# Two transformer blocks in split float32: every SBUF tile begun at a multiple of 128 bytes

## The chip, the cores and the metric

The kernel runs on one core of one Trainium2 chip. The metric is the device time of one execution in microseconds (us), lower is better. The core has five engines with queues of their own: TensorE (PE; its weight loads are listed apart as PEld), VectorE (DVE), ScalarE (ACT), GpSimd (POOL) and SyncE (SP, which issues most of the transfers). A tile of SBUF, the memory on the chip, has up to 128 partitions, and "where a tile begins" is its byte address within each partition.

## The reference, cut to what matters

512 tokens of width 1024 pass two blocks. The first mixes tokens by forgetting attention and gated linear attention, then attends to 256 memory rows, then runs a squared-relu MLP of width 4096. The second runs a SwiGLU layer of width 2816, a mixer of differential attention and of attention over compressed, selected and windowed keys, another SwiGLU layer and a last norm.

```
h = x + parallel_mixer(rms_norm(x, norm_mix_g), ...)          # fox attention | gla, then @ w_out
h = h + memory_cross_attention(rms_norm(h, ...), rms_norm(mem, ...), ...)
u = jax.nn.relu(rms_norm(h, norm_mlp_g) @ mlp_w1)
h = h + (u * u) @ mlp_w2
x = x + 0.5 * swiglu(rmsnorm(x, ffn1_norm), w1, w3, w2)       # (silu(h @ w1) * (h @ w3)) @ w2
x = x + token_mix(rmsnorm(x, mix_norm), w_in, ...)
      # merged = sigmoid(g_a) * (y_da @ w_proj_da) + sigmoid(g_b) * (y_ns @ w_proj_nsa);  merged @ w_out
x = x + 0.5 * swiglu(rmsnorm(x, ffn2_norm), w1, w3, w2)
return rmsnorm(x, final_norm)
```

## The kernel before, in words

Activations are held transposed, 8 tiles of 128 features by 512 tokens. To keep float32's precision at TensorE's single-pass rate, each operand is split into two fp32r tiles: a high part (a copy by ACT) and a low part (DVE subtracts the high part from the full value). A product is then three matmuls: high by high, high by low, low by high. The trace writes fp32r as fp32 or f32. A plain float32 matmul stands as two records there, an fp32r matmul as one.

- `wsub` loads a piece of weights of up to 128x1024 floats (512 KB) into one of 3 `wraw` buffers by SP's queue, and splits every 512 columns of it into one of 4 `wspl` buffers.
- `lin` makes a product with the activations as moving operand: the 128x128 stationary operand comes from `wspl`, the moving operand is 512 columns of x (normed input), u (hidden layer of a MLP), y or z (outputs of attention). `nat` is the other way round: 256 columns of `wspl` move, and 128 columns of x are stationary.
- `norm` makes the tiles x0h, x0l to x7h, x7l in the pool `xp`, which has one buffer for each name, and the norm's factors `rstdb` and `rstdn`.
- Attention streams (`fox`, `gla`, `xattn`, `da`, `nsa`) are woven with streams of projections, so that TensorE has products while a softmax runs on ACT and DVE.

The order on each engine comes from a scheduler that simulates the program's time; the tiles' buffers set what waits for what. Pools are laid out one behind the other, tile behind tile, in steps of 32 bytes. In the built kernel before, the tiles begin this many bytes past a multiple of 128: x, wspl, wraw, misc and nsv 64; u, dav, xv and y (but for four of y in the first mixer, 64) 32; z, kbh and the residual h 96; ones, gc, ident, identr, identb and maskb 0.

At the start, `warm` fills TensorE's wait for the first data with 16 matmuls of `ones` by `ones` (plain float32, 128 columns); then come the gate projection `misc` (64 output rows, over x0 to x7) and the first `nat` products.

Of the kernel before, what the change touches and what calls it, by code (L numbers as in the profile page):

```python
# [31 lines left out]
NGC = _c  # L32


def weave(main, fill, ratio=1.0, lead=0.0):
    """Emit two streams in turn. Each yields the tensor engine's time of what it has emitted, or a
    predicate that the other stream has to make true first."""
# [23 lines left out]
def both(*gens):  # L61
    """generators in turn, in one stream: the second two steps for each of the others"""
    live = [[g, 1] for i, g in enumerate(gens) if g is not None]
    while live:
        for x in list(live):
            for _ in range(x[1]):
                try:
                    v = next(x[0])
                except StopIteration:
                    live.remove(x)  # L70
                    break
                if v is not LATER:
                    yield v


def pipe(gens):
    """generators in one stream, each cut into stages by LATER: a stage comes after the next
    generator's stage before it"""
# [27 lines left out]

class Net:
# [16 lines left out]
    # ---------------------------------------------------------------- small helpers  # L124
# [34 lines left out]
    # ---------------------------------------------------------------- weights  # L159
    def wsub(self, ap, keep=None):  # L160
        """one piece [128, kt, n] of a weight, as its two exact parts: (h, l) of every [128, n]"""
# [18 lines left out]
    def lin(self, w, X, n=S, m=128, parts=None, bank="lin"):  # L180
        """[m, n] = (columns of w)^T X^T; w [128, kt, m] in DRAM, X a list of pairs (None: not yet there)"""
        kt = w.shape[1]
        ps = self.ps(bank)
        i = 0
# [15 lines left out]
    def nat(self, w, X, ntok, evac):  # L200
        """[tok, 256] = X w for w [2, 128, 4, 256]"""
# [14 lines left out]
    # ---------------------------------------------------------------- norms  # L216
    def rsqrt(self, ps, m, d):
        """[128, m]: (ps / d + eps) ** -0.5, with a Newton step"""
# [12 lines left out]
    def token_rsqrt(self, sqs, n, d, sel):  # L231
        """1 / rms over the rows of sqs (per column of sel) of every token; [128 tok, (tile, column)]"""
# [9 lines left out]
    def spread(self, r, n):  # L242
        """[128, n tok] from [128 tok, tile], in PSUM"""
# [11 lines left out]
    def norm(self, h, g, n=S, pool=None, spool=None, first=False):  # L255
        """h: 8 tiles [128, n]; parts of h*g; 1/rms of every token on all partitions, and by token"""
# [28 lines left out]
        rn = spool.tile([128, n // 128], F32, name="rstdn")  # L285
# [3 lines left out]
    def out_proj(self, w, Y, scale=None, banks=("lin",)):  # L289
        """h += (Y w) * scale"""  # L290
# [7 lines left out]
    # ---------------------------------------------------------------- attention pieces  # L298
    def softmax(self, ps, dst, factor=None, scale=True):
        """rows of exp(s - max), times 1/sum (and factor) unless told not to; returns 1/sum"""  # L300
# [18 lines left out]
    def pt(self, P, kbs):  # L319
        """transposed column blocks of a causal P, as parts; where each block begins"""  # L320
# [14 lines left out]
    def av(self, o, P, passes, first, last):  # L335
        """o += sum over key blocks; passes(kb) = [(stationary, part of P)]"""
# [20 lines left out]
    def stacks(self, hi, lo, pool):  # L357
        """[q_hi; q_lo] of the two heads of a tile"""
# [7 lines left out]
    def dup(self, t, U):  # L366
        """each half of the rows on both halves"""
# [5 lines left out]
    def fold(self, ps, dst):  # L373
        """dst [64 rows] = the two halves of an output with parts of V"""
# [4 lines left out]
    def head_tiles(self, w, X, rn, pool, gate, done):  # L379
        """4 heads of 64 columns, by token: 1/rms of each; then transposed, as 2 tiles of 2 heads in PSUM"""  # L380
# [33 lines left out]
    def rope(self, src, dst):  # L414
        """dst = src * cos + (halves swapped) * (-sin, sin)"""
# [12 lines left out]
    # ---------------------------------------------------------------- the whole  # L428
    def run(self):
        tc, nc, a = self.tc, self.nc, self.a  # L430
        with ExitStack() as ctx:
            def pool(name, bufs, c=ctx, side=None):
                kw = {"side": side} if side else {}
                return c.enter_context(tc.tile_pool(name=name, bufs=bufs, **kw))
# [13 lines left out]
            self.small = pool("small", 8)  # L448
            self.stat = pool("stat", 1)
            self.spill = ctx.enter_context(tc.tile_pool(name="spill", bufs=1, space=bass.MemoryType.DRAM))  # L450
            hctx = ExitStack()
            self.hp = pool("hp", 1, hctx, "right")
# [31 lines left out]
    def setup(self):  # L484
# [3 lines left out]
        self.gc = self.const.tile([128, NGC], F32, name="gc")  # L488
        nc.sync.dma_start(self.gc, a["gcols"])
        one = self.const.tile([128, 1], F32, name="one")  # L490
        self.act(one, self.ones[:, 0:1], AF.Exp)
# [14 lines left out]
    def warm(self, n):  # L506
        """keeps the tensor engine's clock up while the first data comes"""
        for _ in range(n):
            self.mm(self.ps("tr")[:, :128], self.ones, self.ones, True, True)

    def late_setup(self):
# [7 lines left out]
        self.gx = self.const.tile([128, 3], F32, name="gx")  # L519
# [3 lines left out]
        self.dah = self.const.tile([128, 8], F32, name="dah")  # L523
# [3 lines left out]
    # ---------------------------------------------------------------- block 1: fox and gla  # L527
    def mixer(self):
        a = self.a
        self.warm(16)  # L530
# [41 lines left out]
    def rowsel(self, pool, rows):  # L572
        """[rows, 8, 128]: -1 where the row is h mod 32"""
# [6 lines left out]
    def log_sigmoids(self, srcs):  # L580
        """log_sigmoid(src + bias) of some (src, bias, rows); all exponentials before the logarithms"""
# [13 lines left out]
    def fox_in(self, X, rb, rn, p1, p2, y, misc):  # L595
        """projections of fox: gates, then keys, queries and values"""
# [3 lines left out]
        def gates():  # L600
# [22 lines left out]
            # log decay of gla, cumulated in every chunk  # L623
# [76 lines left out]
    def gla_proj(self, i, X, rb, rn, p1):  # L700
        """queries, keys and values of two heads of gla"""
# [18 lines left out]
        dd = p1.tile([128, 8], F32, name=f"gdc{i}")  # L720
# [87 lines left out]
    # ---------------------------------------------------------------- block 1: cross attention  # L808
# [104 lines left out]
    # ---------------------------------------------------------------- block 1: mlp  # L913
# [736 lines left out]
```

## Time and profile before

| | |
|---|---|
| three timed runs | 2293.12, 2302.83, 2303.39 us; median 2302.83 |
| profiled execution, first to last instruction | 2294.0 us |
| PE busy | 2256.5 us (98%), 11507 matmul records |
| PEld busy | 1864.0 us (81%) |
| DVE, ACT, POOL busy | 1269.5, 970.9, 245.1 us (55, 42, 11%) |
| chain that ended last, by engine | PE 94%, DVE 2%, ACT 2%, DMA 1%, issue 1% |
| the same by line | `lin` 78%, s 7%, o 4%, transposes 2% |

The chain is followed back from the last instruction, at each step to what released it; its shares say what the time hangs on. No time of the profiled execution other than its span is listed; the span lies 0.9 us above the fastest timed run and 8.8 us below the median. A matmul's start is recorded, its end is modelled, so the rate of a stream is read from starts, not from the duration of one.

### The profile page before, as it was taken

What the parts mean: (1) busy time and instruction counts of PE and PEld (TensorE: products, weight loads), DVE (VectorE), ACT (ScalarE), POOL (GpSimd) and SP (SyncE); (2) the same over time, 40 slices, a digit from 0 to 9 for tenths busy, and PEclk for the clock granted to TensorE, in tenths of its full rate; (3) what the DMA queues carried; (4) which work ended last, traced back from release to release, by engine and by line L of the source; (5) the groups of instructions that cost most, each with busy time, mean ns of one, the idle gap of its engine ahead of it and who ended that gap; (6) DMA issues with size and microseconds to landing.
All of it is one profiled execution on the core that took longest, in us unless ns stands there. A gap on an engine that the chain in (4) does not pass through costs nothing.

```text
span 2294.0 us, 30689 instructions
## 1 busy us (share of the span) xinstructions
PE 2256.5 (98%) x11507; PEld 1864.0 (81%) x11507; DVE 1269.5 (55%) x2397; ACT 970.9 (42%) x1937; POOL 245.1 (11%) x301
## 2 busy tenths in 40 slices
PE   8999999999999999999999999999999999999998
PEld 7887799888888888888878778878877788888887
DVE  6655566655335445435456666677784555543543
ACT  6553355444234333323343334456676334332333
POOL 2201012100000000000002112143441000000000
PEclk9999999999999999999999999999999999999999
DMA  4331133222323322233345455422121322223222
GB/s 141 93 102 51 60 125 107 67 93 93 97 96 95 98 93 92 89 104 99 95 137 134 141 156 139 126 63 62 56 56 63 112 95 99 92 91 102 97 92 79
DMA packets 79268, 222.62 MB, mean 97 GB/s; under 512 B 11536, under 2 KB 19632, under 8 KB 79120
## 3 DMA queue, kind: packets, MB, share of 16 engines
q1 hardware_dynamic: 78480, 220.01, 30.9%
q8 instruction: 90, 1.47, 0.3%
q10 hardware_dynamic: 576, 0.52, 0.1%
q14 instruction: 58, 0.48, 0.1%
q0 software_dynamic: 64, 0.13, 0.0%
HBM read 189.69 MB, written 4.19 MB: 85 GB/s over the span
## 4 chain that ended last, share of the span: by engine, by line
PE 94%; DVE 2%; ACT 2%; DMA 1%; issue 1%; SPq 0%; POOL 0%; ACTq 0%; DVEq 0%; POOLq 0%
PE lin L129 78%; PE s L129 7%; PE o L129 4%; PE tr L326 2%; PE tr L129 2%; DMA wraw<-in_n_vda 0%; ACT P L138 0%; DVE wspl L132 0%; DMA wraw<-in_t_kda 0%; ACT wspl L138 0%; DVE nm L302 0%; ACT pth L138 0%; DVE ta L132 0%; DMA wraw<-in_t_c 0%; ACT L138 0%
## 5 line engine op out<-in xcount | busy, mean ns | idle before, releaser
L138 ACT ACTIVATE wspl<-wraw 128x512 fp32r<-128x512 f32 (+1 forms) x677 | 421.9, 626 | 893.5 <-PE lin L129 802.0
L132 DVE TENSOR_TENSOR wspl<-wraw,wspl 128x512 fp32r<-128x512 f32 (+1 forms) x677 | 469.0, 696 | 442.0 <-ACT wspl L138 434.9
L225 POOL TENSOR_TENSOR rqr<-rqv,mhalf 128x4 f32<-128x4 f32 (+1 forms) x21 | 20.5, 977 | 1386.2 <-DVE rqv L224 1348.7
L129 PE MATMUL lin<-x0h,wspl 128*128 128x512 f32 (+2 forms) x396 | 157.6, 399 | 2.8 <-ACT wspl L138 1.0
L129 PE MATMUL lin<-x7h,wspl 128*128 128x512 f32 (+2 forms) x396 | 153.7, 389 | 0.0
L129 PE MATMUL lin<-x1h,wspl 128*128 128x512 f32 (+2 forms) x396 | 153.7, 389 | 0.0
L129 PE MATMUL lin<-x4h,wspl 128*128 128x512 f32 (+2 forms) x396 | 153.5, 389 | 0.0
L129 PE MATMUL lin<-x6h,wspl 128*128 128x512 f32 (+2 forms) x396 | 153.2, 388 | 0.0
L129 PE MATMUL lin<-x5h,wspl 128*128 128x512 f32 (+2 forms) x396 | 153.2, 388 | 0.0
L129 PE MATMUL lin<-x3h,wspl 128*128 128x512 f32 (+2 forms) x396 | 152.8, 387 | 0.0
L138 ACT ACTIVATE P<-s,nm 128x128 f32<-128x128 f32 (+2 forms) x224 | 117.3, 527 | 83.6 <-DVE nm L302 68.1
L129 PE MATMUL lin<-x2h,wspl 128*128 128x512 f32 (+2 forms) x396 | 152.7, 387 | 0.0
L302 DVE TENSOR_REDUCE nm<-s 128x1 f32<-128x128 f32 (+3 forms) x208 | 105.0, 509 | 53.9 <-PE s L129 52.5
L138 ACT ACTIVATE pth<-tr 128x512 fp32r<-128x512 f32 x152 | 76.4, 529 | 46.4 <-PE tr L326 36.7
L132 DVE TENSOR_TENSOR ptl<-tr,pth 128x512 fp32r<-128x512 f32 x152 | 88.2, 596 | 12.5 <-ACT pth L138 10.5
L129 PEld LDWEIGHTS lin<-x0h,wspl 128*128 128x128 f32 (+1 forms) x396 | 74.9, 189 | 17.4 <-ACT wspl L138 4.2
L129 PEld LDWEIGHTS lin<-x2h,wspl 128*128 128x128 f32 (+1 forms) x396 | 74.5, 188 | 15.2
L129 PEld LDWEIGHTS lin<-x1h,wspl 128*128 128x128 f32 (+1 forms) x396 | 74.8, 189 | 14.8
L129 PEld LDWEIGHTS lin<-x7h,wspl 128*128 128x128 f32 (+1 forms) x396 | 74.4, 188 | 14.8 <-issue 0.2
L129 PEld LDWEIGHTS lin<-x3h,wspl 128*128 128x128 f32 (+1 forms) x396 | 74.3, 188 | 14.9
L129 PEld LDWEIGHTS lin<-x4h,wspl 128*128 128x128 f32 (+1 forms) x396 | 74.5, 188 | 14.6 <-issue 0.2
L129 PEld LDWEIGHTS lin<-x5h,wspl 128*128 128x128 f32 (+1 forms) x396 | 74.4, 188 | 14.5 <-issue 0.2
(705 smaller groups left out, 5550.8 us busy)
## 6 DMA issues: line engine op xcount, KB each, us to landing
wraw<-in_t_m SPq DMA_DIRECT2D x64, 512.0 KB, 3.8
wraw<-in_t_f1a SPq DMA_DIRECT2D x22, 512.0 KB, 3.5
wraw<-in_t_f1b SPq DMA_DIRECT2D x22, 512.0 KB, 3.5
wraw<-in_t_f2a SPq DMA_DIRECT2D x22, 512.0 KB, 3.5
wraw<-in_t_f2b SPq DMA_DIRECT2D x22, 512.0 KB, 3.5
qu<-r SPq DMA_DIRECT2D x80, 128.0 KB, 2.3
wraw<-in_t_f1c SPq DMA_DIRECT2D x16, 512.0 KB, 3.4
wraw<-in_t_f2c SPq DMA_DIRECT2D x16, 512.0 KB, 3.5
```

The source lines that it names most:

```text
L129: self.nc.tensor.matmul(out, lhsT, rhs, start=start, stop=stop, **kw)
L132: self.nc.vector.tensor_tensor(out, in0, in1, op=op)
L138: self.nc.scalar.activation(out, in_, func, **kw)
L225: self.nc.gpsimd.tensor_tensor(r, v, self.mhalf[:, :m], op=OP.pow)
L302: self.nc.vector.tensor_reduce(nm, ps, axis=AX.X, op=OP.max, negate=True)
L326: self.nc.tensor.transpose(ps[:, n:n + 128], P(qb, kb) if callable(P) else P[:, self.po(qb) + kb * 128:self.po(qb) + (kb + 1) * 128], self ...
```

## The change

Allocation: `Lines` wraps every pool but `small` (and the PSUM and DRAM pools). It pads a tile's columns up to a whole number of 128-byte lines, 32 floats or 64 bfloat16. Small fills put the pools themselves on such a line (`SMALLPAD` in `small`, a 24-float tile on the right side), and tiles of a few columns move: rstdn and gdc into `small`, gx, dah and the scratch output `one` into the tail of `gc`. In the built kernel after, every operand of TensorE of 64 columns or more begins at a multiple of 128 bytes; tiles of `small` and three constants begin as before at multiples of 32.

Warming: 8 matmuls of ones instead of 16, then 20 matmuls over zeros whose results nobody reads, with x7h as the moving tile and x7l as the stationary one: 4 of 512 columns, 4 of 448 columns, 4 of 448 columns from column 16 (64 bytes on), 4 of 448 from column 8 (32 bytes on), and 4 in bfloat16 of 512 columns. DVE sets the two tiles to zero first. Comments and docstrings go.

```diff
+SMALLPAD = 24
...
+class Lines:
+    def __init__(self, pool):
+        self.pool = pool
+
+    def tile(self, shape, dtype, name, **kw):
+        step = 64 if dtype == BF16 else 32
+        n = int(np.prod(shape[1:]))
+        if n % step == 0:
+            return self.pool.tile(shape, dtype, name=name, **kw)
+        assert len(shape) == 2
+        return self.pool.tile([shape[0], -(-n // step) * step], dtype, name=name, **kw)[:, :n]
...
-        rn = spool.tile([128, n // 128], F32, name="rstdn")
+        rn = self.small.tile([128, n // 128], F32, name="rstdn", bufs=1) if spool is self.stat \
+            else spool.tile([128, n // 128], F32, name="rstdn")
...
-                return c.enter_context(tc.tile_pool(name=name, bufs=bufs, **kw))
+                return Lines(c.enter_context(tc.tile_pool(name=name, bufs=bufs, **kw)))
...
-            self.small = pool("small", 8)
+            self.small = ctx.enter_context(tc.tile_pool(name="small", bufs=8))
+            self.small.tile([128, SMALLPAD], F32, name="fill", bufs=1)
...
+            ctx.enter_context(tc.tile_pool(name="top", bufs=1, side="right")).tile([128, 24], F32, name="top")
...
-        self.gc = self.const.tile([128, NGC], F32, name="gc")
-        nc.sync.dma_start(self.gc, a["gcols"])
-        one = self.const.tile([128, 1], F32, name="one")
-        self.act(one, self.ones[:, 0:1], AF.Exp)
+        self.gc = self.const.tile([128, NGC + 11], F32, name="gc")
+        nc.sync.dma_start(self.gc[:, :NGC], a["gcols"])
+        self.gx = self.gc[:, NGC:NGC + 3]
+        self.dah = self.gc[:, NGC + 3:NGC + 11]
+        self.act(self.dah[:, 0:1], self.ones[:, 0:1], AF.Exp)
...
             self.mm(self.ps("tr")[:, :128], self.ones, self.ones, True, True)
+        x, w = (self.xp.tile([128, 512], F32R, name=n) for n in ("x7h", "x7l"))
+        self.nc.vector.memset(x.bitcast(F32), 0.0)
+        self.nc.vector.memset(w.bitcast(F32), 0.0)
+        for m, at in ((512, 0), (448, 0), (448, 16), (448, 8)):
+            for i in range(4):
+                self.mm(self.ps("tr")[:, :m], w[:, i * 128:i * 128 + 128], x[:, at:at + m], True, True)
+        for i in range(4):
+            self.mm(self.ps("tr"), w.bitcast(BF16)[:, i * 128:i * 128 + 128], x.bitcast(BF16)[:, :512], True, True)
...
-        self.warm(16)
+        self.warm(8)
```

The scheduler's order changes in the first 60 us or so and hardly anywhere else. On PE before, around the end of the gate projection (`lin<-x7h,wspl 64x512` is its part over the tile x7) and the first transposing sums (`tr<-ones,ta`):

```order
L129 MATMUL lin<-x6l,wspl 64x512
L129 MATMUL lin<-x6h,wspl 64x512
L129 MATMUL lin<-x7h,wspl 64x512
L129 MATMUL tr<-ones,ta 128x1 x4
L129 MATMUL tr<-ones,td 128x1 x4
L129 MATMUL tr<-ones,tb 128x1 x4
L129 MATMUL lin<-x7l,wspl 64x512
L129 MATMUL lin<-x7h,wspl 64x512
L129 MATMUL lin<-wspl,x0h 128x256
```

On PE after, the place where the last test matmul (`tr<-x7h,x7l`) stands, 36 `nat` products (`lin<-wspl,x..`) behind the projection's part over x6:

```order
L145 MATMUL lin<-wspl,x5l 128x256
L145 LDWEIGHTS x7l
L145 MATMUL tr<-x7h,x7l 128x512
L145 MATMUL lin<-wspl,x5h 128x256
L145 MATMUL tr<-ones,ta 128x1 x4
L145 MATMUL tr<-ones,td 128x1 x4
L145 MATMUL tr<-ones,tb 128x1 x4
L145 MATMUL lin<-x7h,wspl 64x512
L145 MATMUL lin<-x7l,wspl 64x512
L145 MATMUL lin<-x7h,wspl 64x512
L145 MATMUL lin<-wspl,x6h 128x256
```

The projection's part over x7 has moved behind the last test and behind the sums. On ACT before, where x7h is written (`tb<-h` are squares for the norm, `spr<-rqo` begins the norm's factor):

```order
L138 ACTIVATE x7h<-h_103,gc 128x512
L138 ACTIVATE tb<-h_103 128x512
L138 ACTIVATE wspl<-wraw 128x512 x3
L138 ACTIVATE sel<-wraw 128x1024
L138 ACTIVATE wspl<-wraw 128x512
L138 ACTIVATE spr<-rqo 128x4
```

and after:

```order
L154 ACTIVATE tb<-h_107 128x512
L154 ACTIVATE wspl<-wraw 128x512 x3
L154 ACTIVATE sel<-wraw 128x1024
L154 ACTIVATE x7h<-h_107,gc 128x512
L154 ACTIVATE wspl<-wraw 128x512
L154 ACTIVATE spr<-rqo 128x4
```

The write of x7h has moved behind four splits, since its buffer is what the tests read.

## Rows read from the trace of the kernel before

**Rows 1.** The page: chain that ended last, by engine and by line.
```profile
PE 94%; DVE 2%; ACT 2%; DMA 1%; issue 1%; SPq 0%; POOL 0%; ACTq 0%; DVEq 0%; POOLq 0%
PE lin L129 78%; PE s L129 7%; PE o L129 4%; PE tr L326 2%; PE tr L129 2%; DMA wraw<-in_n_vda 0%; ACT P L138 0%; DVE wspl L132 0%; DMA wraw<-in_t_kda 0%; ACT wspl L138 0%; DVE nm L302 0%; ACT pth L138 0%; DVE ta L132 0%; DMA wraw<-in_t_c 0%; ACT L138 0%
```
**Rows 2.** The chain's longest pieces: start us, us, what.
```profile
497.67 347.14 PE lin L129 x1508
...
854.06 347.76 PE lin L129 x1518
...
1788.73 137.02 PE lin L129 x593
...
1935.03 338.67 PE lin L129 x1543
```
**Rows 3.** The chain within five stretches: x, u, z; x stationary; u by 256.
```profile
2099.86 118.35 PE lin L129 x522
...
570.75 89.60 PE lin L129 x384
...
1789.85 80.27 PE lin L129 x344
...
1454.43 7.08 PE lin L129 x59
...
2258.45 14.16 PE lin L129 x118
```
**Rows 4.** A window (us, PE busy, PEclk granted, DMA) and the chain inside it.
```profile
1777.40:1783.00 5.60, 5.41 (x12) 0.51 0.13 51
...
1780.19 3.84 PE lin L129 x9
```
**Rows 5.** Timeline and tile ident: eight float32 transposes in a row, one's length.
```profile
59.58 1.04 PE L406 MATMUL tr<-ident,hraw 128*128 128x128 f32 x8
...
L406 PE MATMUL tr<-ident,hraw x32: 270/272/273, 59.6 to 127.1; 128*128 128x128 f32 x32
```
**Rows 6.** Groups by line and form: xcount, then busy us and mean ns.
```profile
L129 PE MATMUL lin<-x1h,wspl 128*128 128x512 f32 x376 | 148.0, 394 | 0.0
L129 PE MATMUL lin<-x1l,wspl 128*128 128x512 f32 x188 | 73.9, 393 | 0.0
L129 PE MATMUL lin<-u2h,wspl 128*128 128x512 f32 x90 | 35.6, 396 | 0.0
L129 PE MATMUL lin<-wspl,x1h 128*128 128x256 f32 x120 | 32.6, 290 | 0.0
...
L129 PE MATMUL lin<-u11h,wspl 128*128 128x512 f32 x32 | 12.7, 396 | 0.0
...
L129 PE MATMUL lin<-x1h,wspl 128*128 128x256 f32 x16 | 4.2, 282 | 0.0
L129 PE MATMUL lin<-u0h,wk 128*128 128x256 f32 x12 | 3.2, 290 | 0.0
```
**Rows 7.** Windows: the first dense stretch, busy us of PE, PEld, DVE, ACT, POOL.
```profile
497.00:845.00 348.00, 348.00 (x1518) 283.98 (x1518) 150.54 (x220) 129.41 (x207) 0.00 (x0) 1.00 0.30 95
```
**Rows 8.** Timeline, the start and one later row: start us, us, engine, [idle before].
```profile
12.76 0.69 PE L129 MATMUL lin<-x3l,wspl 128*64 128x512 f32 x1 [2.23 <-DVE x3l L135]
...
17.12 0.39 PE L129 MATMUL lin<-x7h,wspl 128*64 128x512 f32 x1
...
20.27 0.67 PE L129 MATMUL lin<-x7l,wspl 128*64 128x512 f32 x1
...
21.40 0.63 ACT L138 ACTIVATE wspl<-wraw 128x512 fp32r<-128x512 f32 x1 [3.24 <-PE lin L129]
...
22.06 0.69 DVE L132 TENSOR_TENSOR wspl<-wraw,wspl 128x512 fp32r<-128x512 f32 x1 [1.45 <-ACT wspl L138]
...
25.56 1.00 PE L129 MATMUL tr<-identr,spr 128*128 128x128 f32 x8
...
496.20 0.22 PE L129 MATMUL tr<-identr,spr 128*128 128x128 f32 x1
```

More of the change, by code (lines that the diff above doesn't have):

```diff
@@ L518, in late_setup @@
         nc.gpsimd.tensor_copy(self.maskb, m)
-        self.gx = self.const.tile([128, 3], F32, name="gx")
         nc.vector.tensor_scalar(self.gx[:, 0:1], self.gcol("foxq"), 0.125, None, op0=OP.mult)
@@ L522, in late_setup @@
             nc.vector.tensor_scalar(self.gx[:, 1 + i:2 + i], self.gcol("xq", i), 0.0625, None, op0=OP.mult)
-        self.dah = self.const.tile([128, 8], F32, name="dah")
         c = GCOLS["dah"][0]
@@ L719, in gla_proj @@
         G["kd"][i] = k2
-        dd = p1.tile([128, 8], F32, name=f"gdc{i}")
+        dd = self.small.tile([128, 8], F32, name=f"gdc{i}", bufs=1)
         self.act(dd, c3[:, :, 63], AF.Exp, scale=1.0 / 16)
```

## The prediction

> **What bounds the kernel now.** I read the page's chain first, then its longest pieces, then the rate of single streams, then the granted clock. The chain is TensorE's for 94%, and 78% of the span hangs on `lin`'s and `nat`'s products [rows 1]. Four of its pieces, 1170.6 us and 5162 matmuls together, hold nothing but such products: TensorE waits for nobody there [rows 2]. In the first of them DVE is busy for 150.5 and ACT for 129.4 of 348 us [rows 7]. So the time per matmul is the time of the kernel, and the question is whether it is what it must be.
>
> It isn't, and it isn't the same everywhere. The time from start to start, from the chain's count inside pure stretches [rows 3], is 118.35 / 522 = 226.7 ns with x moving (begins at 64), 89.60 / 384 = 233.3 ns with u (at 32), 80.27 / 344 = 233.3 ns with z (at 96). With 256 columns of wspl (at 64) moving, 7.08 / 59 = 120.0 ns, and with 256 columns of u, 14.16 / 118 = 120.0 ns. At 2.4 GHz, 512 columns are 213.3 ns and 256 are 106.7 ns. So x costs 13.4 ns too much for 512 columns, wspl 13.3 ns too much for 256: the same 32 columns' worth whatever the length, and 32 fp32r columns are 128 bytes of a partition. That is what one looks for when memory is read in lines of 128 bytes and a stream that begins inside a line touches one line more than it holds: 17 for 16, or 9 for 8. u and z pay some 48 columns. In a stretch at the lower level of the clock (granted 0.51 over the window, 1.2 GHz), nine matmuls over z take 3.84 us, 426.7 ns each, exactly 512 columns [rows 4]: nothing is lost there. A fixed cost of TensorE's own would show at both levels; a memory that can just feed one column a cycle at 2.4 GHz shows it only at the higher.
>
> **The change part by part.** *The tiles.* All operands of these streams come to begin on a line. What a 512-column fp32r matmul then costs no row shows, since no such operand begins at 0 now. It lies between the bare columns, 213.3 ns, and what x pays, 226.7 ns. The nearest row is the transposes, whose moving tile ident begins at 0 but is plain float32, which stands in two passes: eight take 1.04 us of which the last is 0.272, so 110 ns for 2 x 53.3 = 106.7, some 2.7 ns on top [rows 5]. I take 216 ns for 512 columns. For 256 columns the same gives 109.4; but the spreading products with identr, of 128 columns, follow each other at (1.00 - 0.22) / 7 = 111 ns (eight, and the length of one, [rows 8]), which may be the weight load's rate, so I take 110.
>
> The Trainium skill, in "TensorE: Matmul & The Clock Gate", section "Wait — 56ns, not 53.3ns?", gives a warm stream N / 2.4 GHz plus about 2.5 ns, 215.8 ns for 512 columns, and ties it to no placement. Our x at 226.7 and u at 233.3 disagree, by 10.9 and 17.5 ns; by it the sum below would come out 2 us larger.
>
> Counts [rows 6]: a tile's high part is in two matmuls, its low part in one, for 8 tiles.
> - x by 512: 8 x (376 + 188) = 4512, by 10.7 ns: 48.3 us.
> - u by 512: 11 tiles x 135 + 5 x 48 = 1725, by 17.3: 29.8 us.
> - z, and y as many, by the code 8 column tiles of weights for two products each: 2 x 8 x 48 = 768, by 17.3: 13.3 us.
> - `nat`: 8 x 180 = 1440, by 10: 14.4 us.
> - x and u by 256: 8 x 24 + 11 x 18 = 390, by 10: 3.9 us.
>
> Together 109.7 us. By the bare columns it would be 134.7; if tiles at 0 pay what those at 64 do, only u, y and z gain 6.6 ns, 16.5 us. The chain is TensorE's for 94%, so I count 103 us. The s and o matmuls of attention, 11% of the chain or 252 us, read tiles at 32 and 96 too; at the same 5% that is 12 us, but most there stand between other waits, and I take 3 us (0 to 12).
>
> ACT and DVE must split weights faster: 150.5 us of DVE would stand in some 326 us instead of 348 [rows 7], still under half. Weight loads are busy for 284 of these 348 us, in 1518 loads, 187 ns each; under 216 ns they stay hidden. Transfers keep the same share of a queue that is 30% busy in the last column but one of [rows 7].
>
> *The padding* moves a few tiles of some columns and adds no instruction that the chain shows; writing gx and dah into gc costs what writing them apart did.
>
> *The tests.* Eight warming matmuls go, 20 tests come. The first 16, some 3.2 us at the full clock and 6.4 at half, stand between the gate projection's parts, where TensorE waits for DVE's low parts today, 2.23 us in one place [rows 8]. What costs is their buffer. x7h and x7l can't be written before the last test has read them, and it stands behind 36 `nat` products. From 17.1 us on, where the projection reaches x7 today [rows 8]: 36 x 0.12 + 4 x 0.22 = 5.2 us, then the sums' 24 records, 2.9 us today (between the x7 parts at 17.12 and 20.27), under which ACT and DVE split x7; the three x7 matmuls, 0.7; then a new wait. The projection's weights hold one of the four wspl buffers, so the last split of the first `nat` weights, 0.63 on ACT and 0.69 on DVE, comes only behind it, 1.4 us with TensorE idle (today other products cover it, [rows 8]); then 12 products, 1.4. The spread starts at 28.7 us instead of 25.56, 3.1 later, with 18 more products (2.2 us) already done. Behind it hang the norm's factor and the gates. I charge 3 us (1 to 3); if the denser stream keeps the clock up, less.
>
> The sum: 2294.0 - 103 - 3 + 3 = 2191 us of span. The profiled execution lies 0.9 us above the fastest run and 8.8 below the median, so timed runs would lie at 2190 to 2200. I forecast **2195 us**.
>
> **The rivals.** *One line stays.* The reader may fetch a line more than it needs even from a line's start, and 13.4 ns be the price of every fp32r stream; then only u, y and z gain: 16.5 x 0.94 - 3 = 12.5 us, 2281 of span, 2285 timed. For it: no fp32r operand of this width begins at 0 today. Against it: 226.7 against 233.3 says that placement counts, and a price that is exactly one line fits a line too many better than one always lost. 0.08.
>
> *Placement isn't the cause*; something that goes with u and z is (which buffers are read at once). Then only the start counts: 2297 of span, about 2300 timed. Against it: x and wspl, of such different sizes and uses, pay the same. 0.05. By the Trainium skill, "SBUF — State Buffer", section "Specifications (TRN2)" (lines of 16 bytes, a penalty for each change of line), this is what should come: a multiple of 32 already begins such a line, so nothing is to be gained by 128. The trace disagrees as far as it goes, 226.7 against 233.3 ns for tiles that all begin on 16 bytes.
>
> *The gain stays in the pure pieces.* In the woven stages another wait ends last as soon as products are shorter. The pure pieces are 1170.6 of the 1794 us of these lines (78.2% of the span): 0.65 x 109.7 = 72 us, less 3, 2225 of span. For it: ACT and DVE waits stand in every softmax. Against it: PE is 94% of the whole chain, and outside the four pieces too `lin` is most of it. 0.08.
>
> *Slower: operands collide.* With every tile at 0, the moving read and the weight load begin at the same place in a line each time and may meet in the same part of the memory. If that costs one line more than x pays now, 240 ns: 4512 x 13.3 + 2493 x 6.7 + 1830 x 13.3 = 101 us, by 0.94 and with the start 2392. It turns slower as soon as an aligned matmul takes more than today's mean of 229 ns. Against it: x and wspl both begin at 64 today, and theirs is the lowest rate; u at 32 with wspl at 64 pays more. 0.04.
>
> **How the numbers follow.** The forecast's own case has 0.75, from 2165 (bare columns, 12 us from attention) to 2220 (a matmul at 220 ns: 4 ns x 7005 = 28 us less). Nearly all of it and the third rival make 0.8, so the range is 2165 to 2240. A measurement of this kernel tells 0.5% (11.5 us) from no change. Faster: 0.75 + 0.08 and most of the first rival's 0.08, 0.90. Same: 0.06. Slower: 0.04.
>
> **What would show it.** In the chain's pieces, 1508 matmuls from about 497 us on should take some 326 us instead of 347, and x, u and z stretches should stand at one rate, 216 ns. The tests say it directly wherever two of a kind follow each other at the full clock: 448 columns at 189 ns from 0, 200 ns (one line more) from 64 bytes on, some 207 ns from 32; 512 columns at 216, in bfloat16 as well. A stretch at the lower clock should stay at 426.7. At the start, x7h is written behind the last test and the spread comes near 28.7 us. I am wrong if x stands at 226.7 still (a line stays), if u and x still differ (not the placement), or if the products shrink and the chain shows DVE or ACT in their place.

## The result, and the profile after

The changed kernel takes 2286.4 us (median of 5, 2279.45 to 2287.58) where the kernel before, timed again beside it, takes 2303.39 (2293.12 to 2304.03). The ratio is 0.9924, 95% interval 0.9901 to 0.9948: 17 us gained, 12 to 23, where I had forecast 108. The profiled execution (2286.07 us, span 2283.5) is close to its median. The spans of the changed kernel's runs lie 1.8 to 2.6 us below their times, so the 2294.0 us of before's span belong to a run of some 2296 us, one of its faster ones: spans understate the gain, and the forecast, which set that span beside timed runs, mixed the two by some 2 us.

The page after, its busy times and its chain by engine and line (the body of `mm` is now L145 instead of L129):

```profile
PE 2249.7 (99%) x11511; PEld 1871.0 (82%) x11511; DVE 1269.5 (56%) x2399; ACT 971.1 (43%) x1937; POOL 243.9 (11%) x301
...
PE 94%; DVE 2%; ACT 1%; DMA 1%; issue 1%; SPq 0%; POOL 0%; DVEq 0%; ACTq 0%; POOLq 0%
```

No other engine has become the bound, as in [rows 1]; DVE's and ACT's work is what it was. The time is still one question, how long a product takes. The chain's four longest pieces after, and below them the chain inside five pure stretches: u, x, z, y, and 256 columns of wspl over a stationary x:

```profile
506.68 341.91 PE lin L145 x1508
857.86 344.15 PE lin L145 x1518
1783.94 134.64 PE lin L145 x593
1927.86 335.75 PE lin L145 x1543
...
579.53 87.04 PE lin L145 x384
2090.25 119.68 PE lin L145 x528
1783.94 81.37 PE lin L145 x358
459.14 30.79 PE lin L145 x135
1448.17 7.32 PE lin L145 x61
```

The stretch of y before, which [rows 3] doesn't hold:

```profile
449.29 31.63 PE lin L129 x135
```

The pieces hold as many matmuls as in [rows 2] and are 5.2, 3.6, 2.4 and 2.9 us shorter, 14.1 together; I had expected the first at 326 and it is 341.91. Inside them u went from 233.3 to 87.04 / 384 = 226.7 ns and z from 233.3 to 81.37 / 358 = 227.3; y went from 31.63 / 135 = 234.3 to 30.79 / 135 = 228.1. But x is at 119.68 / 528 = 226.7 and wspl by 256 at 7.32 / 61 = 120.0, both as in [rows 3]. Everything has come to the rate that x had before, and nothing has gone below it.

The start, as the timeline shows it after (start us, us, engine, idle before):

```profile
19.03 0.39 PE L145 MATMUL tr<-x7h,x7l 128*128 128x512 bf16 x1
...
26.34 0.42 PE L145 MATMUL lin<-x7h,wspl 128*64 128x512 f32 x1
...
27.94 0.39 PE L145 MATMUL lin<-wspl,x6h 128*128 128x256 f32 x1 [0.72 <-ACT wspl L154]
...
30.54 1.64 PE L145 MATMUL tr<-identr,spr 128*128 128x128 f32 x8
```

The scheduler put most tests singly between other products, so they say little here. x7 is late as expected, the new wait is there (0.72 us for the last split, where I had 1.4), and the spread begins at 30.54 us, where I had 28.7 and [rows 8] 25.56. Whether the wait makes it late is asked below.

At 500 us the changed kernel is 9.0 us behind: its first long piece begins at 506.68 us, that of before at 497.67 [rows 2]. The windows show one place where time goes:

```profile
85.00:90.00 5.00, 5.00 (x16) 3.17 (x16) 2.81 (x7) 2.58 (x8) 0.53 (x2) 0.50 0.00 0
```

Here PEclk is 0.50, half the clock (1.2 GHz), for 17.1 us in a row; in the trace of before the clock is at full speed there. In the 5 us from 80 on, around its fall, TensorE was busy for 4.50; so it was from 75 to 80 us in before, where the clock stayed up. Whether the change does that is one of the questions below.

### The profile page after: what moved, and what is told of

Read it like the earlier page. It is cut to its first block, busy times and chain, and to the rows that moved or that the text cites. A ratio compares the mean times of both kernels' runs of the same rounds, so it can differ in the third digit from the quotient of the medians.

```text
span 2283.5 us, 30700 instructions
## 1 busy us (share of the span) xinstructions
PE 2249.7 (99%) x11511; PEld 1871.0 (82%) x11511; DVE 1269.5 (56%) x2399; ACT 971.1 (43%) x1937; POOL 243.9 (11%) x301
## 4 chain that ended last, share of the span: by engine, by line
PE 94%; DVE 2%; ACT 1%; DMA 1%; issue 1%; SPq 0%; POOL 0%; DVEq 0%; ACTq 0%; POOLq 0%
PE lin L145 79%; PE s L145 7%; PE o L145 4%; PE tr L343 2%; PE tr L145 2%; DVE nm L319 0%; DMA wraw<-in_n_vda 0%; ACT P L154 0%; ACT wspl L154 0%; DVE ptl L148 0%; DMA wraw<-in_cw 0%; DVE ta L148 0%; DMA wraw<-in_t_c 0%; DVE wspl L148 0%; DMA h<-in_xT 0%
## 5 line engine op out<-in xcount | busy, mean ns | idle before, releaser
L145 PE MATMUL lin<-x0h,wspl 128*128 128x512 f32 (+2 forms) x396 | 156.8, 397 | 2.8 <-DVE h L148 0.9
L145 PE MATMUL lin<-x6h,wspl 128*128 128x512 f32 (+2 forms) x396 | 153.5, 388 | 0.0
L145 PE MATMUL lin<-x5h,wspl 128*128 128x512 f32 (+2 forms) x396 | 153.4, 388 | 0.0
L145 PE MATMUL lin<-x1h,wspl 128*128 128x512 f32 (+2 forms) x396 | 153.3, 388 | 0.0
L145 PE MATMUL lin<-x2h,wspl 128*128 128x512 f32 (+2 forms) x396 | 153.1, 388 | 0.0
L145 PE MATMUL lin<-x7h,wspl 128*128 128x512 f32 (+2 forms) x396 | 153.1, 387 | 0.0
L145 PE MATMUL lin<-x4h,wspl 128*128 128x512 f32 (+2 forms) x396 | 153.0, 387 | 0.0
L145 PE MATMUL lin<-x3h,wspl 128*128 128x512 f32 (+2 forms) x396 | 152.6, 386 | 0.0
L145 PEld LDWEIGHTS lin<-x0h,wspl 128*128 128x128 f32 (+1 forms) x396 | 74.5, 188 | 17.8 <-ACT wspl L154 3.9
L145 PEld LDWEIGHTS lin<-x2h,wspl 128*128 128x128 f32 (+1 forms) x396 | 74.4, 188 | 15.2
L145 PEld LDWEIGHTS lin<-x3h,wspl 128*128 128x128 f32 (+1 forms) x396 | 74.3, 188 | 15.1
L145 PEld LDWEIGHTS lin<-x1h,wspl 128*128 128x128 f32 (+1 forms) x396 | 74.4, 188 | 14.8
L145 PEld LDWEIGHTS lin<-x6h,wspl 128*128 128x128 f32 (+1 forms) x396 | 74.4, 188 | 14.6 <-issue 0.2
L145 PEld LDWEIGHTS lin<-x5h,wspl 128*128 128x128 f32 (+1 forms) x396 | 74.4, 188 | 14.5
L145 PEld LDWEIGHTS lin<-x7h,wspl 128*128 128x128 f32 (+1 forms) x396 | 74.2, 187 | 14.7 <-issue 0.2
```

Of the source, the lines that this page charges most:

```text
L145: self.nc.tensor.matmul(out, lhsT, rhs, start=start, stop=stop, **kw)
```

## The experiments

All timed ratios are to the kernel before on the same chip. "Place" is a tile's first byte modulo 256. In the built kernel before, wspl and x lie at 192, u at 32, z at 224, y at 32 and 64; after, wspl, u, z, y and most of x lie at 128. Rates of streams are means of the time from start to start at the full clock, where the stream has settled (its first ten or so matmuls take longer); the unused tiles ("shims") only move what is allotted behind them.

### Padding alone, tests alone

`align` is the changed kernel without its tests (16 warming matmuls as before); `tests` is the kernel before with them:

```diff
+        x, w = (self.xp.tile([128, 512], F32R, name=n) for n in ("x7h", "x7l"))
...
-        self.warm(16)
+        self.warm(8)
```

> The padding alone: every tile at a multiple of 128 bytes, with the 16 warming matmuls of before and no tests. Theory 'placement within a line': u, z and y stand at 226.7 ns as x does, none lower, and the start keeps before's times, so the span is 2294 less 16.5 (2493 matmuls by 6.6 ns) less some 3 in attention, 2270 to 2278 us, and the first products after the gates come at the times of before within 1 us. Rival 'the padding costs the start' (tiles moved into gc and small bring waits of their own): the lag of 9 to 12 us that the changed kernel has at 110 us is here too, and the span is 2283 as there.

> The kernel before with the 20 tests in place of 8 warming matmuls, its tiles where they were. Theory 'the tests cost the start': the products behind the gates come 4 to 12 us later than before at 110 us, and the span is 2299 to 2306 us; u stays at 233.3 ns. Rival 'the padding costs the start': no lag, 2294 to 2297 us.

Measured: `align` 2285.62 us, ratio 0.9905 [0.9878, 0.9931]; `tests` 2305.25 us, 1.0001 [0.9981, 1.0021]. The gain is the padding's, all of it, and the tests cost nothing that can be measured (-4 to +5 us). The chain of `align` repeats the changed kernel's pieces to a hundredth of a microsecond, although the first begins elsewhere:

```profile
502.00 341.91 PE lin L145 x1508
853.18 344.15 PE lin L145 x1518
```

So the pieces are a far finer measure than the total, whose runs spread over 6 to 21 us. The span of `align`, 2284.3 us, is above the 2270 to 2278 that I expected: the tiles did as told, the start didn't keep before's times, of which more below.

### u moved off the line by 32 and by 64 bytes

`shim8` (32 bytes) and `shim16` (64 bytes) are `align` with one unused tile ahead of the pool of u in the dense stages:

```diff
+                        c1.enter_context(tc.tile_pool(name="shim", bufs=1)).tile([128, 8], F32, name="shim")
                         self.tmp = pool("tmp", 2, c1)
```

> The padding alone, but a tile of 32 bytes ahead of the pool of temporaries in the dense stages, so that u and the kept weights begin 32 bytes past a line while x and wspl begin on one. Both theories on placement expect u at some 233 ns by 512 columns, 1725 by 6.6 ns or 11.4 us more than with the padding alone. If u stays at 226.7 ns, 32 bytes past a line was not what u paid for.

> The same with 64 bytes: u begins 64 bytes past a line, wspl on one. Theory 'a multiple of 64 bytes is enough': u at 226.7 ns, the time of the padding alone within 3 us. Rival 'it is the place of the moving tile against that of the stationary one' (x and wspl were both at 64, u at 32 against wspl at 64): u pays some 6.6 ns more, 11.4 us in all.

Measured: `shim8` 2300.61 us, 0.998 [0.9958, 1.0003], u back at 233.3 ns; `shim16` 2289.77 us, 0.9932 [0.9906, 0.9958], u at 228.9. x, z and y stay as in `align`. The first piece of the chain of `shim8`:

```profile
500.31 347.12 PE lin L145 x1508
```

and the same piece of `shim16`:

```profile
505.65 343.75 PE lin L145 x1508
```

So it is u's place that pays or costs. But 64 bytes, where x had lain before at 226.7, gives 228.9 to u. "A line of 128 bytes and where the tile begins in it" doesn't explain both.

### Streams of equal matmuls

`probe` is `align` with streams of 32 equal matmuls behind the last norm, over a spare tile Z, each with its own places of the moving (mv) and the stationary (st) operand:

```diff
+        def run(n, mv, st, t=Z, m=128, count=32, k=slice(0, 128)):
+            for _ in range(count):
+                self.mm(ps[:m, :n], t[k, st:st + m], t[k, mv:mv + n], True, True)
+            self.mm(ps[:, :128], self.ones, self.ones, True, True)
```

> The padding alone, and behind the last norm 40 or so streams of 32 equal matmuls over one tile of data, each a stream of its own with a float32 matmul of ones behind it; what they compute is read by nobody, so the time is longer by theirs. Theory 'one line stays' (the reader takes whole lines of 128 bytes and one more than the stream holds): 512 columns of fp32r 226.7 ns at 0, 16, 64 and 128 bytes, more at 32 and 96; 496 columns as 512, 226.7; 480 columns 213.3; bfloat16, which asks for half the bytes, 216. Rival 'a pause per matmul' (13.3 ns between any two fp32r streams, whatever they read): 496 columns 220.0, 480 columns 213.3. Rival 'the stationary operand' (the exchange of 128 fp32r columns of weights costs it): 32 stationary columns instead of 128 bring 512 columns to 216, and the place of the stationary tile changes the time more than that of the moving one. In triples as the products have them (two stationary tiles 2048 bytes apart, two moving ones), the second theory of all: 32 bytes past a line costs 233 on the mean.

Measured, from the timeline: one stream to a row, in the order of the first list below, then widths 384 and 256, and 512 and 256 columns of bfloat16 (its 512 lacks a record).

```profile
2295.45 7.55 PE L145 MATMUL tr<-Z 128*128 128x512 f32 x32
...
2310.61 7.71 PE L145 MATMUL tr<-Z 128*128 128x512 f32 x32
2318.30 7.59 PE L145 MATMUL tr<-Z 128*128 128x512 f32 x32
...
2333.55 7.67 PE L145 MATMUL tr<-Z 128*128 128x512 f32 x32
2341.21 7.70 PE L145 MATMUL tr<-Z 128*128 128x512 f32 x32
...
2356.56 7.52 PE L145 MATMUL tr<-Z 128*128 128x512 f32 x32
...
2408.20 5.81 PE L145 MATMUL tr<-Z 128*128 128x384 f32 x32
2413.99 4.07 PE L145 MATMUL tr<-Z 128*128 128x256 f32 x32
...
2456.36 6.85 PE L145 MATMUL tr<-Z 128*128 128x512 bf16 x31
...
2470.40 3.66 PE L145 MATMUL tr<-Z 128*128 128x256 bf16 x32
```

From start to start, (mv, st) in bytes: (0, 0) 226.7 ns, (32, 0) 233.3, (64, 0) 229.0, (128, 0) 232.4, (0, 64) 233.4, (64, 64) 226.7. In triples as the products have them, two stationary and two moving tiles in turn, the same two rates come: 226.7 at equal places, 233 to 234 at 32 bytes apart. Both operands on a line of 128 bytes can cost 232.4, and both off it 226.7: what counts is where the two lie to each other. At 512 columns that is two prices where I had seen one:

- A fixed one. At equal places 256 columns take 120.0 ns, 384 take 173.3 and 512 take 226.7, 13.3 ns above the bare columns (106.7, 160, 213.3) each. It isn't quite fixed: 448, 480 and 496 columns pay 16.0 to 16.7, so that 496 take 223.3, between the 226.7 of "one line stays" and the 220.0 of a pause. bfloat16 pays little of it: 512 columns 215.8 ns, 256 columns 109.2, and 512 at 32 bytes off as well. Plain float32 takes 429.2 ns a record (two records to a matmul), 2.5 more than twice the bare columns. So it is a price of fp32r. It isn't that of a full stationary tile: 32 stationary columns had 216 ns by that rival, and 64 take 230.0, 32 take 231.7. The Trainium skill, "TensorE: Matmul & The Clock Gate", section "Wait — 56ns, not 53.3ns?", gives N / 2.4 GHz plus some 2.5 ns: that holds here for bfloat16 (215.8 and 109.2 ns) and not for fp32r (226.7 and 120.0).
- One of up to 6.7 ns more, for 512 columns, when the moving tile lies otherwise than its stationary one.

### The tests over other buffers

`own` is the changed kernel with its tests over two ring buffers, so that x7h needn't wait for the last test:

```diff
-        x, w = (self.xp.tile([128, 512], F32R, name=n) for n in ("x7h", "x7l"))
+        x, w = self.R(), self.R()
```

> The changed kernel with the tests over two buffers of the ring r (first needed by fox's queries, far later) instead of x7h and x7l. Theory 'the buffer of x7 holds the start up': x7h is written in its old place, the spread comes near 25.6 us again and the lag at 110 us falls from 12 to 1 to 5 us; the span is 2274 to 2279. Rival 'it is the order and the clock, not the buffer': the lag stays near 9 to 12 us.

Measured: 2282.48 us, 0.9918 [0.9889, 0.9948], against 0.9924 [0.9901, 0.9948] of the changed kernel. The wait on the tests' buffer is worth nothing that can be measured. In its trace the first product over x7h is back at 17.36 us (before 17.12) and the wait of 0.72 us is gone, but the spread begins at 32.29 us and not near 25.6 as expected. The profiled execution has no long stretch at half clock near 85 us and begins its first piece at 498.19 us; its span of 2275.1 lies in the 2274 to 2279 expected, which says as much of the clock as of the buffer.

### Line or relative place, in the kernel

Two kernels on which the theories differ. `bshift` is the kernel before, no padding, with 160 bytes ahead of the pool of u: u lies at 192 like wspl, 64 bytes past a line. `shim32` is `align` with 128 bytes ahead of it: u on a line, 128 from wspl.

```diff
+                        c1.enter_context(tc.tile_pool(name="shim", bufs=1)).tile([128, 40], F32, name="shim")
```

> The kernel before (no padding, no test matmuls, tiles off the 128-byte lines as they were), with one unused tile of 160 bytes ahead of the buffers of u in the dense stages, so that u's tiles move from 32 to 192 modulo 256, where the split weights lie; x, z and y stay where they were. Theory 'the moving tile's place relative to the stationary one': u falls from 233.4 to 226.7 ns though it begins at no line; 1725 such matmuls x 6.7 ns = 11.5 us, so about 2291 us, ratio 0.995. Rival 'a tile must begin at a line of 128 bytes': u begins at 64 modulo 128, stays at 229 to 233 ns, and the ratio is 0.998 to 1.000.

> The padding alone, with one unused tile of 128 bytes ahead of the buffers of u in the dense stages: every tile still begins at a multiple of 128 bytes, but u now lies 128 modulo 256 from the split weights. Theory 'relative place': u at 232.7 ns as in the stream of that difference, x, z and y at 226.7 to 228; 1725 x 6 ns = 10 us of the padding's gain are lost, ratio to before 0.995 instead of 0.9905. Rival 'a line of 128 bytes': u stays at 226.7 ns and the ratio at 0.9905.

Measured: `bshift` 2291.32 us, 0.9949 [0.9929, 0.9969], u at 226.7 ns; `shim32` 2299.68 us, 0.9984 [0.9964, 1.0004], u at 233.3. The chain's pieces in `bshift`:

```profile
508.81 341.91 PE lin L129 x1508
...
1787.44 137.03 PE lin L129 x593
1933.76 335.74 PE lin L129 x1543
```

and in `shim32`:

```profile
502.76 347.05 PE lin L145 x1508
...
1794.27 134.64 PE lin L145 x593
1938.19 338.62 PE lin L145 x1543
```

An unused tile of 160 bytes, in both dense stages, gives the pieces over u all that the padding gave (341.91 us, 335.74), off every line; the piece over z, which it doesn't move, stays at the 137.03 of before. And 128 bytes in the padded kernel put the pieces over u back to what they were before (347.05, 338.62), on a line, while z keeps its gain. The line is out. For `shim32` I had taken 232.7 ns from the stream; 233.3 were paid, so 11.4 us of the padding's gain go and not 10. Its ratio lies above the 0.995 that I expected even so: I had counted from `align`'s 0.9905, the lowest of the three padded kernels, and from the changed kernel's 0.9924 these 11.4 us lead to 0.997.

### A map of places

`probe2`, the same streams with the stationary tile in steps behind the place of the moving one, then pairs of matmuls in turn:

```diff
+        for st in (4, 8, 12, 16, 24, 32, 40, 48, 56, 64, 96, 128, 192):
+            run(512, 0, S0 + st)
+        for mv, st in ((32, 32), (32, 96), (64, 0), (100, 36)):
+            run(512, mv, S0 + st)
...
+        pairs(((Z, S0, 0), (Z, S0 + 8, 8)))
+        pairs(((Z, S0, 8), (Z, S0 + 8, 0)))
```

> The padding alone, and behind the last norm streams of 32 equal float32r matmuls of 512 columns over a spare tile, that leave the outputs as they are. First a map: the moving tile fixed, the stationary one 16, 32, 48, 64, 96, 128, 160, 192, 224, 256, 384, 512 and 768 bytes behind an equal place. Theory 'relative place modulo 256': 226.7 ns at 256, 512 and 768 again, 229 to 233.5 at all between, 232.7 at 128 and 384. Rival 'relative place modulo 512': 256 and 768 near 233, 512 at 226.7. Both tiles moved by 128 bytes: 226.7 by the theory. Then two stationary tiles in turn: with each matmul 0 from its own and 32 bytes from the next one's, and the other way round. If the load of the next weights meets the stream, the first pays 233 and the second 226.7; if a matmul's own weights count, the reverse. Then float32r and bf16 in turn: if the 13.3 ns that a float32r matmul pays at equal places come from the load of the next float32r weights, the float32r stream with bf16 weights next to come takes 220 or less and the bf16 stream with float32r weights next more than 216; if they are the float32r stream's own, it stays at 226.7 and bf16 at 215.8.

The streams 32, 128, 192, 256, 384 and 512 bytes apart, and both tiles moved by 128:

```profile
2295.38 7.71 PE L145 MATMUL tr<-Z 128*128 128x512 f32 x32
...
2326.15 7.68 PE L145 MATMUL tr<-Z 128*128 128x512 f32 x32
...
2341.49 7.58 PE L145 MATMUL tr<-Z 128*128 128x512 f32 x32
...
2356.74 7.55 PE L145 MATMUL tr<-Z 128*128 128x512 f32 x32
2364.26 7.68 PE L145 MATMUL tr<-Z 128*128 128x512 f32 x32
2371.92 7.55 PE L145 MATMUL tr<-Z 128*128 128x512 f32 x32
...
2386.97 7.52 PE L145 MATMUL tr<-Z 128*128 128x512 f32 x32
```

and, behind them, 256 columns with the moving tile 32 bytes on:

```profile
2460.04 3.99 PE L145 MATMUL tr<-Z 128*128 128x256 f32 x32
```

The period is 256 bytes: 226.7 ns at 256, 512 and 768 (the first ten matmuls, before the stream is in step, make the 7.55), 232.4 at 128 and 384, 229.0 at 192 and 233 to 234 at the rest. In both this map and the last one 229 belongs to a moving tile 64 bytes ahead of its stationary one modulo 256, which is also where `shim16` put u, at 228.9. All this is for 512 columns. The same program has narrower streams with the moving tile 32 bytes on: 448 columns take 204.4 ns against 202.7 at equal places, 384 take 173.3 in either, and 256 take 116.7 against 120.0, so that there equal places are the slower ones. The pairs kept neither promise: two matmuls in turn, each at its own stationary tile's place and 32 bytes from the next one's, took 231.8 ns each; the other way round 230.0. And fp32r and bfloat16 in turn took 460 ns a pair, 17.5 more than the two apart, whatever the places, so that pair says nothing of the fixed price.

### All the products, without padding

`rel` is `bshift` with z (32 bytes) and the y of the cross-attention (160) moved to 192 as well:

```diff
+        self.newpool("shim", 1, self.ph).tile([128, 40], F32, name="shim")
         y = self.newpool("y", 1, self.ph)
...
+                        self.newpool("shim", 1, l1, "right").tile([128, 8], F32, name="shim")
                         zp = self.newpool("zp", 1, l1, "right")
```

> The kernel before without padding and without tests, with three unused tiles that move u (160 bytes), z (32 bytes) and the y of the cross-attention (160 bytes) to 192 modulo 256, where the split weights lie; the y of the first mixer stays. No tile that it moves begins at a multiple of 128 bytes. Theory 'relative place': u, z and that y at 226.7 to 228 ns; 1725 x 6.7 + 384 x 6.6 + 192 x 6.9 ns = 11.6 + 2.5 + 1.3 = 15.4 us, so about 2288 us, ratio 0.9933, which is within a microsecond or two of what all the padding brings. Rival 'the padding has a part of its own beside the place' (the tiles of the other engines, the narrow matmuls): the moved streams are as fast, but the ratio stays clearly above the padding's 0.9905.

Measured: 2289.23 us, 0.9939 [0.9916, 0.9963]; u 226.7 ns, z 226.8, that y 227.6, the y that stayed 233 to 234. Its pieces are the changed kernel's:

```profile
508.10 341.91 PE lin L129 x1508
...
1785.39 134.64 PE lin L129 x593
1929.32 335.74 PE lin L129 x1543
```

Unused tiles of 160 and 32 bytes do for these products what padding every pool did. No part of the padding's own is seen: the interval holds the 0.9924 of the changed kernel and overlaps that of the padding alone (0.9878 to 0.9931). None of `align`, `own` and `rel` can be told from the changed kernel, so no version is put forward as faster.

### What a single displacement costs

`probe3`: rows of seven equal matmuls and one that differs, six times over; then places of a few bytes, and narrow streams.

```diff
+        same = [(Z, S0, 0)] * 7
+        rows(same + [(Z, S0 + 8, 0)], 6)
+        rows(same + [(Z, S0, 8)], 6)
+        rows(same + [(Z, S0 + 8, 8)], 6)
...
+        rows(same + [(Z, S0 + 256, 512)], 6)
```

> The padding alone, and behind the last norm streams over a spare tile. Rows of seven equal float32r matmuls at equal places (226.7 ns each) and one that differs, six times over: its stationary tile, its moving tile, or both, displaced by 32 bytes, its stationary tile by 128, or both parts far away at equal places, or its type bf16. Theory 'the load of the next weights meets the stream': a displaced stationary tile lengthens the one matmul before its own, a displaced moving tile its own only, both displaced lengthen the one before (its stream against the displaced weights) and their own (their stream against the next weights). Rival 'a matmul's own stationary tile': only the displaced one is longer, and both displaced cost nothing. Both far away at equal places: 226.7 in either. Then places of 4 and 8 bytes beside the stationary tile and equal places that begin at 16, 32, 48, 64 and 96 bytes: where both begin off a multiple of 32 bytes 230 as the last map had, otherwise 226.7. Then 320, 192 and 128 columns: with a fixed price of 13.3 ns beside the columns 146.7, 93.3 and 66.7; with a price per column 142, 85 and 57.

The first three rows of 48 and the one with equal far places, then equal places 16 and 32 bytes on, then 320, 192 and 128 columns and 128 of bfloat16:

```profile
2301.86 11.27 PE L145 MATMUL tr<-Z 128*128 128x512 f32 x48
2313.11 11.32 PE L145 MATMUL tr<-Z 128*128 128x512 f32 x48
2324.41 11.30 PE L145 MATMUL tr<-Z 128*128 128x512 f32 x48
...
2346.92 11.18 PE L145 MATMUL tr<-Z 128*128 128x512 f32 x48
...
2392.40 7.71 PE L145 MATMUL tr<-Z 128*128 128x512 f32 x32
2400.09 7.54 PE L145 MATMUL tr<-Z 128*128 128x512 f32 x32
...
2430.24 4.93 PE L145 MATMUL tr<-Z 128*128 128x320 f32 x32
2435.15 3.79 PE L145 MATMUL tr<-Z 128*128 128x192 f32 x32
2438.95 3.77 PE L145 MATMUL tr<-Z 128*128 128x128 f32 x32
2442.82 1.95 PE L145 MATMUL tr<-Z 128*128 128x128 bf16 x32
```

Both theories on which matmul pays fall. One stationary tile displaced by 32 bytes makes several longer (a settled group of eight reads 226, 227, 227, 226, 235, 229, 232, 231 ns from start to start), 19 ns in all; a displaced moving tile costs some 30, both displaced some 26, and both far away at equal places nothing. A stream takes some matmuls to fall back into step, so the price isn't one of a single matmul and its own or its next weights. Equal places aren't quite enough either: both tiles 16 bytes on gave 233.3 ns where I had expected 230, both 48 bytes on 230.1; at the multiples of 32 it is 226.7. The fixed price is confirmed at 320 columns, 146.7 ns; at 192 and 128 columns fp32r stands at 111.7 ns for either, far from the 93.3 and 66.7 expected and so another limit, where bfloat16 takes 55.8 for 128.

### The start

No run is about the start alone, but `align`, `probe`, `probe2` and `probe3` are one and the same program up to the last norm. Their first long piece begins at 502.00, 505.95, 495.31 and 505.77 us. The same window as above in `probe`:

```profile
85.00:90.00 5.00, 5.00 (x17) 3.23 (x16) 3.11 (x7) 2.70 (x7) 1.06 (x2) 0.50 0.00 0
```

and in `probe2`:

```profile
85.00:90.00 5.00, 5.00 (x36) 4.09 (x35) 4.39 (x11) 4.57 (x13) 0.93 (x3) 1.00 0.00 0
```

The stretch at half clock comes and goes between executions of the same instructions: before the first piece half clock was granted for 37.5 us in `probe` and 13.7 in `probe2`, and the piece began 10.6 us apart. The same stretch stands in `bshift` and `rel`, which run before's own order of products up to there, without padding or tests: half clock for 37.5 us where before's trace has 13.7, and first pieces at 508.81 and 508.10 us, 11 us behind before's. The changed kernel has 34.1 us; as an estimate, a product takes 426.7 ns at half clock [rows 4] and some 230 at full, so 20.4 us more of half clock cost some 9.4 us, and it is 9.0 us behind. `tests` has 30.7 us and begins the piece at 508.12; its span of 2301.8 us is what I expected of tests that cost the start, but the clock makes nearly as much. So the lag is as large as the clock alone makes it, and no part of it is shown to be the change's. Nor is the late spread: in `rel` it begins at 30.10 us, in `probe2`, without tests, at 25.74 and in `probe` at 29.26. The granted clock varies on one chip too, and the span with it: of `align`'s six runs two have a mean granted clock of 0.993 and spans of 2271.4 and 2275.4 us, the other four 0.986 to 0.988 and 2282.8 to 2284.8.

## Why the prediction was wrong, step by step

**What bounds the kernel**: right. TensorE's products did and do, no other engine took over, and the gain stands where the products are.

**The tiles** are the step that failed: "It lies between the bare columns, 213.3 ns, and what x pays, 226.7 ns", and then "I take 216 ns for 512 columns". It is 226.7, the upper of the two bounds, and 120 for 256 columns where I took 110. The forecast came from two readings. The first, that the excess is "the same 32 columns' worth whatever the length" and therefore a line of 128 bytes read in vain: a price that doesn't depend on the length is as well a price per matmul, and that is what the widths show (146.7 ns at 320 columns, 226.7 at 512, at equal places). That nothing of it is seen at half clock, which I held against a cost of TensorE's own, doesn't decide it: no run shows that such a cost must stand at both levels. The second was to take the transposes' 110 ns in plain float32 [rows 5] as the nearest row for fp32r: float32 and bfloat16 don't pay the price, fp32r does, so the row was near in place and far in the thing that counts. In the sum this takes the 48.3 us of x, 14.4 of `nat` and 3.9 of the narrow products, 66.6 of 109.7, to nothing, and the 43.1 of u, z and y to 1725 x 6.7 + 384 x 6.0 + 384 x 6.2 = 16.2 us, with the one stretch of y taken for all of it. The measured gain is 17 (12 to 23).

**The counts** were right: u and z make 13.9 of the 16.2 us, and the four pieces, which hold nearly all of them, are 14.1 shorter. The share of 0.94 wasn't put to the test by that, since almost all that became faster stands in these pieces.

**The padding** costs nothing that shows: DVE 1269.5 us before and after, `align` as fast as the changed kernel.

**The tests** were charged with 3 us. The order and the wait came as told, the wait with 0.72 us instead of 1.4. That it moves the spread didn't hold: 30.54 us is close to the 30.10 that `rel` has without tests, and `own`, without the wait, has 32.29. `tests` alone is at 1.0001 and `own` can't be told from the changed kernel: at most 5 us, and nothing shown.

**The rivals.** "One line stays" gave 2285 us and 6.6 ns for u, y and z alone, and 2286.4 came. Its number was right by luck; its reason wasn't. No line is the unit: a tile on a line pays 233.3 (`shim32`), one off it 226.7 (`bshift`). Padding every tile to 128 bytes helped because it left wspl, u, z and y at the same place modulo 256, which nothing in it asks for: that too is luck. The rate of x before was low for the same reason, it lay where wspl lay. "Operands collide" named the right two tiles, the moving and the stationary one, with the wrong sign: at 512 columns equal places are the best. I had the evidence in it, "u at 32 with wspl at 64 pays more", and used it only to dismiss that rival. "Placement isn't the cause" falls for u, y and z. For x it is right in that no place tried was faster at 512 columns; for `nat` and the products by 256 it isn't shown, since the one stream of 256 columns with a displaced tile was faster, 116.7 against 120.0 ns, a gain that the padding doesn't reach for. This rival drew on the Trainium skill, "SBUF — State Buffer", section "Specifications (TRN2)", where lines are of 16 bytes: by that alone u at 32 should have nothing to gain, and 233.3 against 226.7 ns says that it had.

**Open.** What makes the 13.3 ns of an fp32r matmul at equal places; why 32 bytes of displacement slow 512 columns and quicken 256; and what meets what in the up to 6.7 ns (the 256 bytes, the 229 at 64 bytes one way only, the slow return into step). It is shown that the places of the moving and the stationary tile decide it, in the kernel and in streams, not by which reading they do.

## What to carry to other kernels

When two streams of the same matmul run at different rates, compare the places of both operands, moving and stationary, not of one, and try the cheapest displacement of one pool before padding all of them; here 160 bytes gave 11.7 of the 14.1 us that the four pieces gained. Try it at the width that the kernel uses: what helped at 512 columns didn't at 256. A constant excess over lengths may as well be a price per instruction: ask a stream of another width and another type before giving it a cause in memory. And where the total spreads by 10 us between executions of one program, compare pieces of the chain with equal counts: those here repeat to 0.1 us.

## What the runs showed of the hardware

- An fp32r matmul at full clock and equal places takes 13.3 ns more than its columns at 256, 320, 384 and 512 columns and 16.0 to 16.7 at 448 to 496, bfloat16 2.5 at 256 and 512; at the half clock of [rows 4] nothing is seen of it.
- Moving against stationary place, modulo 256 bytes, 512 columns of fp32r: 226.7 ns at 0, 229.0 with the moving tile 64 ahead, 232 to 234 at the other multiples of 16 tried. With the moving tile 32 ahead: 204.4 against 202.7 ns at 448 columns, 173.3 in either at 384, 116.7 against 120.0 at 256. bfloat16 and plain float32 show no such price at 32 bytes (215.8 and 429.2 ns, as at 0).
- fp32r and bfloat16 in turn take 460 ns a pair instead of 442.5.
- fp32r products of 128 and of 192 columns both take 111.7 ns, bfloat16 of 128 columns 55.8.
- The same instructions were granted half clock (1.2 GHz) for 13.7 us of the first 495 in one execution and for 37.5 of the first 506 in another, and were 10.6 us apart by then.
